# Layer 0's FFN: three pairs by token halves and eight by seven products, with six products ahead of the second projection and zeros between the convolution's additions

## The chip, the core and the metric

The kernel runs on one core of one Trainium2 chip. The core has five engines with a queue of instructions each: TensorE (PE, matmuls; its weight loads are shown as PEld), VectorE (DVE), ScalarE (ACT), GpSimd (POOL) and SyncE (SP, which here only issues DMAs). The metric is the device time in microseconds (us), the median of several runs. Lower is better.

## The reference

A two-layer decoder trunk on 512 tokens of width 1024, all in float32. Layer 0 is a causal convolution module and a SwiGLU FFN; layer 1 is sliding-window attention and the same kind of FFN. What matters here is layer 0:

```python
def swiglu_ffn(x, w_up, w_down):
    gate, up = jnp.split(x @ w_up, 2, axis=-1)
    return (jax.nn.silu(gate) * up) @ w_down

def conformer_conv(x, w_pw1, b_pw1, w_dw, b_dw, ln_g, ln_b, w_pw2, b_pw2):
    a = jax.nn.glu(x @ w_pw1 + b_pw1, axis=-1)
    y = lax.conv_general_dilated(
        a, w_dw[:, None, :].astype(a.dtype), window_strides=(1,),
        padding=((CONV_WIDTH - 1, 0),),
        dimension_numbers=('NWC', 'WIO', 'NWC'),
        feature_group_count=D_MODEL) + b_dw
    y = jax.nn.silu(layernorm(y, ln_g, ln_b))
    return y @ w_pw2 + b_pw2

h = x
h = h + conformer_conv(rmsnorm(h, norm_mix[0]), ...)
h = h + swiglu_ffn(rmsnorm(h, norm_ffn[0]), ffn_w_up[0], ffn_w_down[0])
...
```

The convolution is 31 taps wide. `w_up` is 1024 x 5632 and `w_down` 2816 x 1024, so the FFN's hidden width is 2816: 22 tiles of 128, which the kernel takes as 11 pairs.

## The kernel before, in words

**Layout.** Channels lie on the partitions, tokens along the free axis. `h` is eight tiles of 128 x 512. The tokens are also worked on as two halves of 256 (`HALF`).

**Weights.** All weights come as chunks of 128 x 1024 (512 KB) in one order, `PLAN`, made by `chunk_plan` (L92). SP loads a chunk into one of six `raw` buffers (`load`, L257), up to nine ahead. `split_weights` (L293) then splits it, three ahead, into a rounded part `whi` (ACT, L294) and the rest `wlo` (DVE, L297), with four buffers each, and a matmul of such operands is three (`mm3`, L376): whi by x's high part, whi by x's low part, wlo by x's high part, on L380 to L382. Chunks up to pair 0 of part 0 (`NATIVE`) aren't split (L378). `advance` (L299) does all of this and runs once for each chunk used; `get` (L362) calls it, and also `pace` (L337), which counts gets and brings background jobs as far as their points say. A point (get, step) means: so many steps by that get.

**Two ways through the FFN's up projection.** Before the change pairs 0 to 3 go *by token halves* (`HALVES0[0]`): `ffn_part` runs once for the first 256 tokens (part 0; three matmuls of 256 columns per step) and once for the second (part 1, `twin`; `mm2`, L407: one matmul of 512 columns, high and low parts side by side, and one of 256). Each part runs four up chunks per pair and, after all its pairs, two down chunks per pair. Pairs 4 to 10 go *by seven products* (Strassen-Winograd over two halves of the input channels and two halves of the tokens; `SEVEN`, L57): seven chunks per pair for all 512 tokens, each a `product` (L801) of 24 matmuls of 256 columns. Their weight blocks A11 to A22 are in memory; the sums S1 to S4 are made in DRAM by `prepare` (L277), a fraction `share[0]` of a sum per chunk: SP copies a block (`copy_sums`, L269; the first nine pairs' in bulk while the convolution runs), and POOL's DMA queue adds a second block onto it (L289). The token sums T1 to T4 are made by `Rows0.sums` (L1284). `SevenPair.take` (L818) evacuates each product into a tile `c`, and `gates` (L844) finishes the pair: DVE L849 and L852, silu on ACT L850, multiplication on POOL L853.

**Order of layer 0.** The convolution of the first token half; pw2 for it; part 0 (ups, then downs); three products A12 ahead of their pairs (`FIRST`: they need only the first half's tokens), kept in a `quad`; pw2 for the second half; part 1; the other products of pairs 4 to 10; all 14 of their down chunks; then the shared K/V projection.

**The second half's convolution** (`Half`, L976) runs in the background of pw2 and part 0. Taps are shared: DVE accumulates 14 to 16 of each channel tile's 31 (L1009); for the others ACT multiplies (L1001) and POOL adds (L1002). After the last tap POOL joins the two (L1013), ACT squares (L1038), PE sums over the channels (`sums`, L1058), `scales_a` turns the sums (PE L1067, then small DVE operations), `scales_b` makes the scales (POOL L1080, ACT L1085), `spread` broadcasts them (PE L1089), and `rows` makes the eight tiles z (DVE L1101 and L1102, ACT L1103, split L544 and L545), which the second pw2 reads. Each of these is a step of the job at L1243; 39 steps of taps are left when it starts, so the squares are step 40, the sums 44, the scales 45 and 46, the spread with the first row 49, the last row 56. The order on each engine is fixed when the kernel is built; `issue_after` keeps an instruction from being placed ahead of another.

Outputs of part 0's downs are added into `h` by L621 and L622, of part 1's by L604 to L607 (L606 on POOL), of the seven-product pairs' by L1356. An up pair of part 0 is evacuated by L659, L661, L662 and `split` (L544, L545).

Of the kernel before, what the change touches and what calls it, by code (L numbers as in the profile page):

```python
# [34 lines left out]
HALVES0 = ((0, 4), (4, 11))  # L35
FIRST = (4, 5, 6)
# [38 lines left out]
def part2_products():  # L75

    steps, held = [], []
    for pair in range(*HALVES0[1]):
# [13 lines left out]
def chunk_plan():  # L92
# [19 lines left out]
    plan.extend(("up0", *step) for step in part2_products())  # L112
    downs(*HALVES0[1])
# [96 lines left out]
def hybrid_trunk(ctx: ExitStack, tc: tile.TileContext, xT, W, prm_in, wdw_in, sinks, relb, onehot, fin, lead, out):  # L210
# [53 lines left out]

    def pool_op(op):
        pooled[0] = op.ins
        return op
# [107 lines left out]

    def mm3(out, w, x, start, stop, **kw):  # L376
# [4 lines left out]
        nc.tensor.matmul(out, w[0], x[1], start=False, stop=False, **kw)  # L381
        nc.tensor.matmul(out, w[1], x[0], start=False, stop=stop, **kw)  # L382
# [202 lines left out]
    def ffn_part(layer, part, xg, tok, rms, on_h=None, twin=False, plain=None):  # L585
# [3 lines left out]
        for g in range(2):  # L589
            if twin:  # L590
# [210 lines left out]
    def product(key, block, r, opens, closes=True):  # L801
# [131 lines left out]

    with tc.tile_pool(name="conv", bufs=2) as cv:
# [41 lines left out]
        class Half:  # L976
# [7 lines left out]
            def taps(self, ct, c):  # L984
# [9 lines left out]
                for i in range(nd):  # L994
                    while pi * nd < n_pool * (i + 1):
# [4 lines left out]
                        else:  # L1000
                            on_act = nc.scalar.mul(pr, a[:, j:j + W2], tap(j))  # L1001
                            on_pool = pool_op(nc.gpsimd.tensor_add(pr, acc, pr))  # L1002
# [105 lines left out]
            def background(self):  # L1108
# [24 lines left out]
                self.spread()  # L1133
# [109 lines left out]
        job(second, (base, 0), (base + 8, 19), (base + 13, 22), (base + 26, 40), (base + 30, 45), (base + 34, 50), (base + 35, h1.n_steps - early - 3))  # L1243
# [28 lines left out]
    class Rows0:  # L1272
# [11 lines left out]
        def sums(self):  # L1284
# [6 lines left out]
            for n, (name, t, f, a, b) in enumerate((  # L1291
# [12 lines left out]
                both = z0.tile([P, 2, 4, 256], F32R, tag="z0", name=uid("rows"), bufs=5)  # L1304
# [5 lines left out]
    z0 = part2.enter_context(tc.tile_pool(name="part2", bufs=5))  # L1310
    plain1 = z0.tile([P, KT, W2], F32, tag="z0", name=uid("plain1"), bufs=5)
# [7 lines left out]
    flush()  # L1319
# [3 lines left out]
    share[0] = 1 / 4  # L1323
    lo0, hi0 = HALVES0[1]
    hid0, open_pairs = [], {}
    left = [n for n, _ in part2_products()]
    for pair, a in part2_products():
        if pair not in open_pairs:
            c = z0.tile([P, 2, 2, 2, 256], F32, tag="z0", name=uid("up"), bufs=5)
            open_pairs[pair] = SevenPair("up0", pair, rows0, c, first.get(pair))  # L1330
        open_pairs[pair].take(a)
        left.remove(pair)
        if pair in left:
            continue
        c = open_pairs[pair].gates()
        if 2 * (pair - lo0) == len(hid0):
            if pair == hi0 - 1:
                q = quad()
                two = q[:, 0:2], q[:, 2:4]
            else:  # L1340
                two = quad(), quad()
            hid0 += [[d[:, k, :] for d in two] for k in range(two[0].shape[1])]
        for m in range(2):
            split([d.rearrange("p (s q) -> p s q", s=2) for d in hid0[2 * (pair - lo0) + m]], c[:, m, :, 0, :])
    part2.close()

    attn = ExitStack()
    at = attn.enter_context(tc.tile_pool(name="attn", bufs=2))
    job(chain(*(read_bias(*b) for b in ((0, 0), (0, 1), (1, 0)))), (seen[0], 0), (seen[0] + 10, 7))
    share[0] = 0.6  # L1350
    if True:
# [346 lines left out]
```

## Time and profile before

| | |
|---|---|
| median of 3 runs | 1043.42 us (1043.19 to 1044.5) |
| profiled execution | 1043.27 us, its span 1041.5 us |
| mean granted TensorE clock | 0.997 |
| busy share of the span: PE, PEld, DVE, ACT, POOL | 99%, 90%, 75%, 59%, 45% |
| DMA | 248.33 MB, mean 238 GB/s |

The profile is of one execution. A group's row gives line, engine, operation, names and shapes, the count, busy us and the mean ns of one, then the engine's idle time before these instructions and what ended it. The chain of waits is followed back from the last instruction; in order of time it shows when each piece starts and how long it holds the chain. The sums by stage give each engine's busy time in a stretch. Layer 0's stages by the trace: first pw2 from about 129 us, part 0 from 158, the three early products from 235, the second pw2 from 244, part 1 from 267, the seven products from 339, their downs from 474 to 550.

### The profile page before, as it was taken

What the parts mean: (1) busy time and instruction counts of PE and PEld (TensorE: products, weight loads), DVE (VectorE), ACT (ScalarE), POOL (GpSimd) and SP (SyncE); (2) the same over time, 40 slices, a digit from 0 to 9 for tenths busy, and PEclk for the clock granted to TensorE, in tenths of its full rate; (3) what the DMA queues carried; (4) which work ended last, traced back from release to release, by engine and by line L of the source; (5) the groups of instructions that cost most, each with busy time, mean ns of one, the idle gap of its engine ahead of it and who ended that gap; (6) DMA issues with size and microseconds to landing.
All of it is one profiled execution on the core that took longest, in us unless ns stands there. A gap on an engine that the chain in (4) does not pass through costs nothing.

```text
span 1041.5 us, 17709 instructions
## 1 busy us (share of the span) xinstructions
PE 1031.5 (99%) x6580; PEld 932.6 (90%) x6580; DVE 776.5 (75%) x1202; ACT 613.0 (59%) x1062; POOL 473.2 (45%) x569
## 2 busy tenths in 40 slices
PE   9999999999999999999999999999999999999996
PEld 8888889999988999998888877788989999898995
DVE  3999989978789777673536566678686877868777
ACT  3887798847776556552333565466655556554654
POOL 3999999930535233221214255405442334434134
PEclk9999999999999999999999999999999999999998
DMA  9999747999999988999969766955879988877742
GB/s 356 340 315 207 205 126 204 272 256 275 249 239 262 304 220 284 256 301 244 286 209 254 210 183 183 228 154 152 252 230 312 287 264 264 245 233 222 224 150 81
DMA packets 67282, 248.33 MB, mean 238 GB/s; under 512 B 7579, under 2 KB 13884, under 8 KB 66364
## 3 DMA queue, kind: packets, MB, share of 16 engines
q1 hardware_dynamic: 54236, 200.75, 55.9%
q0 software_dynamic: 12672, 46.14, 24.8%
q8 instruction: 51, 0.84, 0.3%
q10 hardware_dynamic: 288, 0.31, 0.1%
q14 instruction: 35, 0.29, 0.1%
HBM read 241.93 MB, written 97.52 MB: 326 GB/s over the span
## 4 chain that ended last, share of the span: by engine, by line
PE 98%; DMA 0%; DVE 0%; issue 0%; POOLq 0%; SPq 0%; POOL 0%; ACT 0%
PE bank L380 20%; PE bank L382 20%; PE bank L381 20%; PE bank L960 10%; PE bank L902 9%; PE bank L412 4%; PE bank L378 4%; PE bank L413 2%; PE bank L1441 1%; PE bank L1483 1%; PE bank L1470 1%; PE bank L1058 1%; PE bank L1607 1%; PE bank L948 1%; DMA both<-in_lead_dram 0%; PE bank L1562 0%
## 5 line engine op out<-in xcount | busy, mean ns | idle before, releaser
L297 DVE TENSOR_TENSOR wlo<-raw,whi 128x1024 fp32r<-128x1024 f32 x246 | 329.7, 1348 | 136.8 <-ACT whi L294 136.5
L294 ACT CAST whi<-raw 128x1024 fp32r<-128x1024 f32 x246 | 257.1, 1049 | 276.6 <-PE bank L381 194.1
L380 PE MATMUL bank<-quad,whi 128*128 128x256 f32 (+1 forms) x976 | 307.4, 317 | 0.0
L381 PE MATMUL bank<-quad,whi 128*128 128x256 f32 (+1 forms) x976 | 306.6, 315 | 0.0
L382 PE MATMUL bank<-quad,wlo 128*128 128x256 f32 (+1 forms) x976 | 305.7, 315 | 0.0
L380 PEld LDWEIGHTS bank<-quad,whi 128*128 128x128 f32 x976 | 185.5, 191 | 12.8 <-issue 1.6
L381 PEld LDWEIGHTS bank<-quad,whi 128*128 128x128 f32 x976 | 186.0, 191 | 11.9 <-issue 0.5
L382 PEld LDWEIGHTS bank<-quad,wlo 128*128 128x128 f32 x976 | 185.6, 191 | 11.8 <-issue 0.4
L853 POOL TENSOR_TENSOR up<-up 128x512 f32<-128x512 f32 x34 | 62.9, 1851 | 283.6 <-ACT up L850 283.6
L1002 POOL TENSOR_TENSOR pr<-pr,pr 128x256 f32<-128x256 f32 x208 | 155.4, 788 | 2.6 <-ACT pr L1001 2.5
L380 PE MATMUL bank<-rows,whi 128*128 128x256 f32 x488 | 138.0, 283 | 0.0
L381 PE MATMUL bank<-rows,whi 128*128 128x256 f32 x488 | 137.8, 282 | 0.0
L382 PE MATMUL bank<-rows,wlo 128*128 128x256 f32 x488 | 137.8, 282 | 0.0
L1009 DVE SCALAR_TENSOR_TENSOR bank<-apad,wdw,bank 128x256 f32<-128x256 f32 x248 | 112.4, 485 | 3.4
L1001 ACT ACTIVATE pr<-apad,wdw 128x256 f32<-128x256 f32 x208 | 98.3, 502 | 14.9 <-POOL pr L1002 13.1
L960 PE MATMUL bank<-quad,w 128*128 128x256 f32 x448 | 98.7, 380 | 0.0
L960 PEld LDWEIGHTS bank<-quad,w 128*128 128x128 f32 x448 | 84.9, 190 | 11.8 <-DVE bank L1009 0.2
L380 PEld LDWEIGHTS bank<-rows,whi 128*128 128x128 f32 x488 | 93.1, 191 | 0.3
L381 PEld LDWEIGHTS bank<-rows,whi 128*128 128x128 f32 x488 | 93.1, 191 | 0.3
L382 PEld LDWEIGHTS bank<-rows,wlo 128*128 128x128 f32 x488 | 93.0, 191 | 0.0
L491 POOL TENSOR_TENSOR tmp<-tmp,tmp 128x256 f32<-128x256 f32 (+1 forms) x28 | 26.8, 957 | 101.4 <-ACT tmp L487 96.2
L412 PE MATMUL bank<-quad,whi 128*128 128x512 f32 x168 | 59.7, 398 | 0.0
(230 smaller groups left out, 1635.9 us busy)
## 6 DMA issues: line engine op xcount, KB each, us to landing
raw<-in_W_dram SPq DMA_DIRECT2D x170, 512.0 KB, 5.7
raw<-sum SPq DMA_DIRECT2D x88, 512.0 KB, 5.4
sum<-in_W_dram SPq DMA_DIRECT2D x52, 512.0 KB, 6.2
sum<-in_W_dram POOLq DMA_DIRECT2D x44, 512.0 KB, 9.6
sum<-sum POOLq DMA_DIRECT2D x44, 512.0 KB, 8.5
sum<-in_W_dram SPq DMA_DIRECT2D x4, 3584.0 KB, 30.4
w<-in_W_dram SPq DMA_DIRECT2D x14, 512.0 KB, 8.6
sum<-in_W_dram SPq DMA_DIRECT2D x4, 1024.0 KB, 30.3
```

The lines of the kernel that those rows point to most:

```text
L294: on_act = nc.scalar.copy(hi, src).ins
L297: latest[:] = [on_act, lo_engine[0].tensor_sub(lo, src, f32(hi)).ins]
L380: nc.tensor.matmul(out, w[0], x[0], start=start, stop=False, **kw)
L381: nc.tensor.matmul(out, w[0], x[1], start=False, stop=False, **kw)
L382: nc.tensor.matmul(out, w[1], x[0], start=False, stop=stop, **kw)
L412: nc.tensor.matmul(first[2], first[0], first[1], start=start, stop=False)
L853: pool_op(nc.gpsimd.tensor_mul(gate, gate, c[:, m, :, 1, :]))
L902: nc.tensor.matmul(out, x, w[:, ws], start=first and e == 0 and i == 0, stop=e == 1 and i == 2, skip_group_check=True)
L960: mm = nc.tensor.matmul(self.pb[:, w * W2:(w + 1) * W2], w1_of(ct, w, k), x[k] if x else xg[k][:, tok], start=k == 0, stop=k == KT - 1)
L1001: on_act = nc.scalar.mul(pr, a[:, j:j + W2], tap(j))
L1002: on_pool = pool_op(nc.gpsimd.tensor_add(pr, acc, pr))
L1009: on_dve = nc.vector.scalar_tensor_tensor(yt if i == nd - 1 else c, src, tap(i), c if i else self.shift, op0=ALU.mult, op1=ALU.add)
```

## The change

Pair 3 goes by seven products, so that three pairs go by halves and eight by products. The products run in two groups of four pairs (`GROUPS0`), each followed by its own down chunks, with the outputs added into `h` after each. The products A12 of six pairs (3 to 8) instead of three run ahead of the second pw2, with two gets counted by `pace` in each; two of their results lie in a new pool `keep`. `part2`'s pool has four buffers instead of five, and the tile `c` of odd pairs is a `quad`. From the second half's job on, each POOL addition of the convolution, and L606, is followed by a memset of 128 x 64 zeros into a tile that nobody reads. The job's points are new, and its sums, scales and spread are not placed ahead of the last matmul of `mm3` (`stamp`). The shares of sums per chunk become 0.5 (was 0.45) ahead of the products and 0.45 (was 0.25) among them. `EARLY` follows from `PLAN`: eight units in the first bulk copy instead of seven, one in the second instead of two.

```diff
-HALVES0 = ((0, 4), (4, 11))
-FIRST = (4, 5, 6)
+HALVES0 = ((0, 3), (3, 11))
+GROUPS0 = ((3, 7), (7, 11))
+FIRST = tuple(range(3, 9))
...
-    plan.extend(("up0", *step) for step in part2_products())
-    downs(*HALVES0[1])
+    for group in GROUPS0:
+        plan.extend(("up0", *step) for step in part2_products(group))
+        downs(*group)
...
+    letting = []
+
     def pool_op(op):
         pooled[0] = op.ins
+        return op
+
+    def let_go(op):
+        if letting:
+            with tc.issue_after(op.ins):
+                pool_op(nc.gpsimd.memset(letting[0], 0.0))
         return op
...
-            nc.tensor.matmul(out, w[0], x, start=start, stop=stop)
+            stamp[0] = nc.tensor.matmul(out, w[0], x, start=start, stop=stop).ins
...
-        nc.tensor.matmul(out, w[1], x[0], start=False, stop=stop, **kw)
+        stamp[0] = nc.tensor.matmul(out, w[1], x[0], start=False, stop=stop, **kw).ins
...
-                    pool_op(nc.gpsimd.tensor_mul(t, t, rs_bc))
+                    let_go(pool_op(nc.gpsimd.tensor_mul(t, t, rs_bc)))
...
         for which in range(2):
+            if which and between is not None:
+                between()
...
-                            on_pool = pool_op(nc.gpsimd.tensor_add(pr, acc, pr))
+                            on_pool = let_go(pool_op(nc.gpsimd.tensor_add(pr, acc, pr)))
...
                 for n, (_, f) in enumerate(due):
-                    f()
+                    with tc.issue_after(stamp[0]):
+                        f()
...
-                self.scales_a()
+                with tc.issue_after(stamp[0]):
+                    self.scales_a()
...
-                self.spread()
+                with tc.issue_after(stamp[0]):
+                    self.spread()
...
-        job(second, (base, 0), (base + 8, 19), (base + 13, 22), (base + 26, 40), (base + 30, 45), (base + 34, 50), (base + 35, h1.n_steps - early - 3))
+        letting.append(cpool.tile([P, 64], F32, tag="letting", name="letting"))
+        job(second, (base, 0), (base + 8, 19), (base + 13, 22), (base + 24, 39), (base + 28, 43), (base + 29, 44), (base + 30, 44),
+            (base + 31, 46), (base + 33, 48), (base + 34, 49), (base + 37, h1.n_steps - early))
...
-        preparing[0], share[0] = prepare(), 0.45
+        preparing[0], share[0] = prepare(), 0.5
...
-        first = quad(F32)
-        first = {pair: first[:, n, :].rearrange("p (a s) -> p a s", a=2) for n, pair in enumerate(FIRST)}
+        first = [quad(F32)] + [keep.tile([P, 512], F32, tag="c11", name=uid("c11")) for _ in FIRST[4:]]
...
-            product(("up0", pair, "A12"), [[x0["ffn0"][4 + k][e][:, HALF[0]] for k in range(4)] for e in range(2)], r, True)
+            product(("up0", pair, "A12"), [[x0["ffn0"][4 + k][e][:, HALF[0]] for k in range(4)] for e in range(2)], r, True, pace)
...
-    job(rows0.sums(), (base + 11, 0), (base + 19, 8), (base + 26, 14), (base + 32, 17))
+    job(rows0.sums(), (base + 10, 0), (base + 16, 8), (base + 22, 12), (base + 27, 14), (base + 31, 17))
...
-    share[0] = 1 / 4
-    lo0, hi0 = HALVES0[1]
-    hid0, open_pairs = [], {}
-    left = [n for n, _ in part2_products()]
-    for pair, a in part2_products():
+    share[0] = 0.45
+    for group in GROUPS0:
+        lo0, hi0 = group
+        last = hi0 == HALVES0[1][1]
+        hid0, open_pairs = [], {}
+        left = [n for n, _ in part2_products(group)]
+        for pair, a in part2_products(group):
+            if pair not in open_pairs:
+                if pair % 2:
+                    c = quads.tile([P, 2, 2, 2, 256], F32, tag="quad", name=uid("up"))
...
+            pace()
+            open_pairs[pair].take(a)
...
         for g in range(2):
             banks = accs(512)
             down_group([(("down", 0, kp, g), 2 * (kp - lo0)) for kp in range(lo0, hi0)], lambda kt: hid0[kt], banks)
             for m in range(4):
                 nc.vector.tensor_add(h[g * 4 + m], banks[m], h[g * 4 + m])
-                nxt.on_h(g * 4 + m)
+                if last:
+                    nxt.on_h(g * 4 + m)
```

More of the change, by code (lines that the diff above doesn't have):

```diff
@@ L72, in blocks_of, with part2_products @@
     return [(kind, pair, n.split()[0]) for n in SEVEN]
-def part2_products():
+def part2_products(group):
     steps, held = [], []
-    for pair in range(*HALVES0[1]):
+    for pair in range(*group):
         names = [n.split()[0] for n in SEVEN]
@@ L799, in hybrid_trunk, with product @@
     PARTNER = dict(n.split() for n in SEVEN)
-    def product(key, block, r, opens, closes=True):
+    def product(key, block, r, opens, between=None):
         w = [x.rearrange("p (a k c) -> p a k c", a=2, k=4) for x in get_seven(*key)]
         for which in range(2):
+            if which and between is not None:
+                between()
             for k in range(4):
@@ L932, in norm_x @@
         return pb
+    kept = ExitStack()
+    keep = kept.enter_context(tc.tile_pool(name="keep", bufs=max(1, len(FIRST) - 4)))
     with tc.tile_pool(name="conv", bufs=2) as cv:
@@ L1248, in hybrid_trunk @@
         pw2(h0.z, n0)
-        preparing[0], share[0] = prepare(), 0.45
+        preparing[0], share[0] = prepare(), 0.5
         ffn_part(0, 0, x0["ffn0"], HALF[0], n0.rms, plain=plain)
-        first = quad(F32)
-        first = {pair: first[:, n, :].rearrange("p (a s) -> p a s", a=2) for n, pair in enumerate(FIRST)}
+        first = [quad(F32)] + [keep.tile([P, 512], F32, tag="c11", name=uid("c11")) for _ in FIRST[4:]]
+        first = {pair: t.rearrange("p (a s) -> p a s", a=2)
+                 for pair, t in zip(FIRST, [first[0][:, n, :] for n in range(4)] + first[1:])}
         for pair in FIRST:
@@ L1345, in hybrid_trunk @@
[L1345 to L1351, printed above, removed]
+    share[0] = 0.45
[8 more added lines that the diff above has]
+                    c = quads.tile([P, 2, 2, 2, 256], F32, tag="quad", name=uid("up"))
+                else:
+                    c = z0.tile([P, 2, 2, 2, 256], F32, tag="z0", name=uid("up"), bufs=4)
+                open_pairs[pair] = SevenPair("up0", pair, rows0, c, first.get(pair))
+            pace()
+            open_pairs[pair].take(a)
+            left.remove(pair)
+            if pair in left:
+                continue
+            c = open_pairs[pair].gates()
+            if 2 * (pair - lo0) == len(hid0):
+                if pair == hi0 - 1:
+                    q = quad()
+                    two = q[:, 0:2], q[:, 2:4]
+                else:
+                    two = quad(), quad()
+                hid0 += [[d[:, k, :] for d in two] for k in range(two[0].shape[1])]
+            for m in range(2):
+                split([d.rearrange("p (s q) -> p s q", s=2) for d in hid0[2 * (pair - lo0) + m]], c[:, m, :, 0, :])
+        flush()
+        if last:
+            part2.close()
+            kept.close()
+            attn = ExitStack()
+            at = attn.enter_context(tc.tile_pool(name="attn", bufs=2))
+            job(chain(*(read_bias(*b) for b in ((0, 0), (0, 1), (1, 0)))), (seen[0], 0), (seen[0] + 7, 7))
+            share[0] = 0.6
@@ L1356, in hybrid_trunk @@
                 nc.vector.tensor_add(h[g * 4 + m], banks[m], h[g * 4 + m])
-                nxt.on_h(g * 4 + m)
+                if last:
+                    nxt.on_h(g * 4 + m)
+    if True:
         x, rms = nxt.x, nxt.rms
```

25 lines of the change are left out of this document (4 added, 21 removed).

## The prediction

> **What bounds the kernel now.** I read the page first, then the chain of waits, then sums by stage.
>
> ```profile
> span 1041.5 us, 17709 instructions
> ...
> PE 1031.5 (99%) x6580; PEld 932.6 (90%) x6580; DVE 776.5 (75%) x1202; ACT 613.0 (59%) x1062; POOL 473.2 (45%) x569
> ...
> PE 98%; DMA 0%; DVE 0%; issue 0%; POOLq 0%; SPq 0%; POOL 0%; ACT 0%
> ```
>
> PE alone carries the chain. The profiled execution took 1043.27 us, 1.77 outside its span; the median of the runs is 1043.42, so the sum below is made against 1043.27. A busy PE row doesn't show how long one matmul holds the chain; the chain in order of time does (start, length):
>
> ```profile
> 396.29 0.12 PE bank L381
> 396.41 0.12 PE bank L382
> ...
> 399.17 0.12 PE bank L381
> ```
> ```profile
> 287.85 0.23 PE bank L412
> 288.08 0.12 PE bank L413
> 288.20 0.23 PE bank L412
> ```
> ```profile
> 479.20 0.23 PE bank L382
> ...
> 479.88 0.23 PE bank L382
> ```
>
> A 256-column matmul costs 0.12 us: a product (24 of them; the first and last row are 24 apart) 2.88. The token-half step of part 1 (512 and 256 columns, L412 and L413) costs 0.35, its chunk of eight 2.80. A 512-column matmul costs 0.68 / 3 = 0.227, a chunk of 24 of them 5.44. Nobody else bounds a stage, but two come near (columns: stretch, its length, then busy us of PE, PEld, DVE, ACT, POOL, then clock, DMA share, GB/s):
>
> ```profile
> 172.00:208.50 36.50, 36.50 (x300) 36.29 (x299) 34.23 (x47) 28.17 (x52) 34.66 (x39) 1.00 0.99 271
> 208.50:234.50 26.00, 26.00 (x212) 25.76 (x211) 19.33 (x30) 11.93 (x18) 8.29 (x10) 1.00 0.92 255
> 243.70:339.00 95.30, 95.30 (x616) 86.50 (x616) 82.59 (x106) 64.87 (x109) 36.66 (x37) 1.00 0.92 255
> 339.00:474.00 135.00, 135.00 (x1105) 133.76 (x1104) 96.51 (x109) 74.51 (x98) 35.66 (x26) 1.00 0.91 274
> 474.00:550.50 76.50, 76.50 (x339) 63.32 (x339) 33.63 (x34) 28.83 (x40) 18.40 (x20) 1.00 0.80 236
> ```
>
> From 172 to 208.5, where the second half's convolution runs under part 0 of the FFN, DVE is busy 94%, POOL 95%, and DMA is full. The granted clock is 1.00 throughout, so no clock term.
>
> **The PE sum.** Pair 3 leaves the halves. Part 0 loses four up and two down chunks, 6 x 2.88 = 17.28 (24 matmuls of 256 columns each, the product's price); part 1 loses 6 x 2.80 = 16.80. Added are seven products, 7 x 2.88 = 20.16, and two down chunks, 2 x 5.44 = 10.88. Sum: 31.04 - 34.08 = **-3.04 us**. The products A12 of pairs 7 and 8 only move forward; the cut into two groups adds no matmul. PE shows no idle to win back, so -3.04 is about the floor, and the question is what stalls come.
>
> **The tight place: the second half's LayerNorm.** Before the second pw2, part 0 gets 6 x 2.88 shorter and 3 x 2.88 longer: 8.64 us less cover for a chain that runs convolution, column sums, spread, z. Today's chain (four views; rows in time):
>
> ```profile
> 206.84 1.86 POOL L1002 TENSOR_TENSOR pr<-pr,pr 128x256 f32<-128x256 f32 x2
> 216.54 2.42 POOL L1013 TENSOR_TENSOR y<-y,pr 128x256 f32<-128x256 f32 x2 [7.84 <-DVE y L1009]
> ```
> ```profile
> 215.92 0.87 DVE L1009 SCALAR_TENSOR_TENSOR y<-apad,wdw,bank 128x256 f32<-128x256 f32 x2
> 251.83 0.75 DVE L545 TENSOR_TENSOR quad<-tmp,quad 128x256 fp32r<-128x256 f32 x2
> ```
> ```profile
> 219.00 0.42 ACT L1038 ACTIVATE sq<-y 128x256 f32<-128x256 f32 x1 [1.26 <-POOL y L1013]
> ```
> ```profile
> 220.31 1.73 PE bank L1058 x8
> 225.15 0.79 PE bank L1067 x8
> 234.44 0.86 PE bank L1089 x2
> ```
>
> POOL's additions end at 208.70 and then wait 7.84 for DVE, whose taps end at 216.79; 2.6 us on, at 219.42, the sums can start, and PE takes them at 220.31. The spread ends at 235.3, three products follow, and pw2 starts at about 243.9; its last z lands at 252.58, when the fourth pw2 chunk (243.9 + 8.64 = 252.5) begins. There is no room to spare today.
>
> After: pw2 starts at 243.9 - 8.64 = 235.3. Going back over five products (14.40), spread, scales and sums (0.86 + 0.79 + 1.73), the sums stand at 217.5, ahead of the second product. So the taps must be done by 217.5 - 2.6 = 214.9, 1.9 sooner than today. With the added gets (two per product) the steps run 1.55 per get instead of 1.38, and the taps end at get 24, one earlier. DVE's order up to there loses one weight split and pair 3's evacuation (L659, L662, L545) and takes in the first half of the down evacuation (L621 and L622, twice each), all like this row (columns here and next: count, busy, mean ns):
>
> ```profile
> L662 DVE TENSOR_TENSOR bank<-bank,tmp 128x512 f32<-128x512 f32 x4 | 2.7, 687 | 0.0
> L297 DVE TENSOR_TENSOR wlo<-raw,whi 128x1024 fp32r<-128x1024 f32 x18 | 28.1, 1572 | 2.1 <-ACT whi L294 2.1
> ```
> ```profile
> L297 DVE TENSOR_TENSOR wlo<-raw,whi 128x1024 fp32r<-128x1024 f32 x11 | 13.5, 1223 | 4.3 <-ACT whi L294 4.2
> ```
> ```profile
> L1002 POOL TENSOR_TENSOR pr<-pr,pr 128x256 f32<-128x256 f32 x40 | 38.1, 1010 | 1.8 <-ACT pr L1001 1.8
> ```
> ```profile
> L1002 POOL TENSOR_TENSOR pr<-pr,pr 128x256 f32<-128x256 f32 x34 | 23.5, 730 | 0.0
> ```
>
> That is -1.57 - 3 x 0.69 + 4 x 0.69 = -0.9: taps at 215.9, 1.0 too late if nothing else changes. The rows show what may change: a split takes 1.572 from 160 to 217, where POOL adds, but 1.223 from 240 to 270, where it doesn't; an addition takes 1.010 beside the splits and 0.730 from 100 to 125 without them. The two engines block each other; the splits alone lose 18 x 0.35 = 6.3 us. Zeros between the additions could let DVE in. The relief isn't measured: between 0 and 6.3; I take a third, 2.1, because a split that meets a running addition must still wait for it, and only double waits vanish. Then the taps end at 213.8 and the sums wait for nothing.
>
> By the Trainium skill (SBUF — State Buffer, § Who interferes with whom) a DVE instruction with two SBUF inputs contends with a GpSimd instruction that reads SBUF, not with one that only writes. The trace agrees as far as the split's two durations go, and by that rule alone the relief is whole: taps at 209.6, the total still the PE sum, 1040.2. The same page (§ SBUF: two separate sides) lets whichever starts first keep the pair for its whole instruction, which speaks against the change, since the zeros shorten no addition under way: relief near 0, which gives the third case below.
>
> POOL pays for the zeros. Of the 116 additions of this half, 54 are emitted early, so 62 get one (and eight in L606, off this chain). Of 64 columns there is no row; nearest are these (the second: seven of 30 columns, so (0.47 - 0.12) / 6 = 0.058 each):
>
> ```profile
> 1.08 0.20 POOL L469 MEMSET mean_m<- 128x128 f32 x1
> ...
> 1.81 0.47 POOL L937 MEMSET apad<- 128x30 f32 x7
> ```
>
> So 3.6 to 12.4 us; between the two by width, 0.107, makes 6.6: additions end at 215.3, and with two y additions of 0.73 and the square the sums are ready at 217.2 against 217.5. The 7.84 us of POOL idle are eaten almost whole. I allow **0.2 us** of PE waiting, here or at the z. The z: DVE needs about 8 us for eight rows (three steps of 0.33) with splits taking 1.22 of every 2.88, some 14 us from the spread's end (217.5 + 1.73 + 2.88 + 0.79 + 2.88 + 1.44 + 0.86 = 228.1), so 242.1, against 243.9 needed. Behind a late sum or spread, everything on PE queues, since its order is fixed.
>
> **The rest, hidden.** Eight more evacuations between the groups (0.69 each) lie under down chunks, where DVE is busy 33.63 of 76.5; uncovered, the next product would wait for a bank, at most four of them, 2.7 us. Three more PSUM copies on ACT replace others in part 2. T1 to T4 come at gets 17 to 29 instead of 20 to 32; the first product that needs one of them is get 28, and T4's own is get 33. Part 1 keeps DVE's 87%: six splits and a pair go with the time. The POOL multiplication that closes each group's last pair has three down chunks, 16 us, ahead of its use.
>
> DMA is where the change asks for more: sums at 0.45 per chunk in part 2 instead of 0.25 (SP's queue carries the loads and the copies, POOL's the accumulations). Between 120 and 560:
>
> ```profile
> q1 hardware_dynamic: 21839, 83.46, 53.1%
> q0 software_dynamic: 6912, 25.17, 32.3%
> ...
> raw<-in_W_dram SPq DMA_DIRECT2D x105, 512.0 KB, 5.9
> ```
> ```profile
> ACT whi L294 <- DMA raw<-in_W_dram: 4.4, 1, 4.4
> ```
>
> 512 KB cost 0.531 x 440 / 159 = 1.47 us of all DMA engines on q1, 0.323 x 440 / 48 = 2.96 on q0. Part 2 now needs 1.47 + 0.25 x 4.43 = 2.58 per 2.88, or 0.90, and the row says 0.91. After: 1.47 + 0.45 x 4.43 = 3.46, that is 1.20, in the second group's 26 products: 15 us behind at their end. Loads start it with six raw buffers full and four chunks split, over 20 us ahead, and the down chunks give it back; ACT waited only once for a load, though DMA stood at 0.99. I count nothing.
>
> **Forecast and rivals.** 1043.27 - 3.04 + 0.2 = **1040.4**. About 0.2%, 2.1 us, can be told from no change.
> 1. All but a little of the PE sum arrives: 1039.6 to 1041.3. Chance 0.56.
> 2. POOL becomes the last ahead of the sums: at 0.20 per zero the additions end at 221.1, the sums are ready at 223.0, PE waits 5.5: 1045.7, more if the zeros also slow the additions. Slower than before from a wait of 3.04, or about 0.16 per zero. For it speaks POOL's 95%, against it the short row of 30 columns. 0.15.
> 3. The zeros do not do what they are for: DVE stays blocked, the sums are 1.0 late, and the last z, which today lands as it is used, as much again: 1042.2. DVE's 94% speaks for it. 0.19.
> 4. DMA holds the loads in the second group: if the six raw buffers alone cover, six products (17.3) less a landing (5.9) and the two halves of a split (2.3) make 9, and 15 less 9 is 6: 1046.2. The full share speaks for it, the single wait against. 0.10.
>
> So faster 0.56, same 0.19, slower 0.25. The range is 1039.4 to 1046.5, which takes in most of the second and fourth; the first alone is 1039.6 to 1041.3.
>
> **What would show it.** The products at 2.88 and 50 of them in part 2; L1002's mean down from 1.010 or L297's from 1.572 under the convolution; zeros near 0.1 us; no PE gap ahead of L1058, L1067, L1089 and the second pw2; DMA share about 1 in the second group without ACT waiting for raw. A gap of over 1 us at one of these places, or at the weights in the second group, makes it wrong.

## The result, and the profile after

The changed kernel takes 1051.31 us (median of 6 runs, 1050.92 to 1052.44), the kernel before 1043.61 beside it: a ratio of 1.0076, with a 95% interval of 1.0063 to 1.0089. It is slower, by 7.7 us; 1040.4 was forecast. The profiled execution took 1051.06, 7.79 above that of before. Line numbers have moved: a weight split on DVE is now L307 (was L297), an addition of the convolution on POOL L1018 (L1002), an accumulation's issue L299 (L289), and the zeros are L276. The page of the changed kernel, its span, engines and chain:

```profile
span 1049.0 us, 17719 instructions
...
PE 1033.1 (98%) x6556; PEld 933.1 (89%) x6556; DVE 780.6 (74%) x1208; ACT 611.3 (58%) x1059; POOL 488.0 (47%) x643
...
PE 86%; DVE 5%; issue 3%; POOL 2%; ACT 2%; DMA 0%; POOLq 0%; ACTq 0%; DVEq 0%
```

PE has 24 matmuls fewer and is no longer alone on the chain of waits: DVE, POOL and ACT are on it for 9% of the span. The view of waits for PE, 120 to 560 us (us in total, times, longest), has no row in the kernel before and three after:

```profile
PE bank L541 <- ACT tmp L527: 2.9, 1, 2.9
PE bank L393 <- DVE quad L557: 2.7, 3, 2.2
PE bank L392 <- DVE up L844: 0.9, 1, 0.9
```

The first is under part 0, and so is the second but for 0.2 us in the second pw2; the third is at the start of part 2. The chain of waits ahead of the first (start, length):

```profile
178.69 0.70 POOL sq L1060
179.39 0.10 POOL letting L276
179.54 0.16 POOL letting L276
179.75 0.16 POOL letting L276
...
180.65 1.88 POOL sum L299 x2
182.52 0.16 POOL letting L276
182.68 0.69 POOL rs L519
...
183.70 0.39 ACT tmp L527
```

Part 0's RMS scale goes through four engines: DVE makes the mean square `ms` (L517), POOL a power of it, `rs` (L519), ACT a diagonal (L527), and PE spreads that (L541). POOL's rs stands in POOL's queue behind a group of six zeros and two accumulations (L299). DVE's ms was ready long before (first row); in the kernel before, rs (there L507, second row) ran 4 us earlier:

```profile
175.91 0.15 DVE L517 TENSOR_SCALAR ms<-bank 128x2 f32<-128x2 f32 x1
```
```profile
178.61 0.71 POOL L507 TENSOR_TENSOR rs<-ms,mhalf 128x2 f32<-128x2 f32 x1
```

So the first wait comes from POOL's queue: ms ended at 176.06, and rs held the chain from 182.68. DVE's timeline shows the second wait:

```profile
191.85 5.83 DVE L307 TENSOR_TENSOR wlo<-raw,whi 128x1024 fp32r<-128x1024 f32 x1
...
202.25 1.28 DVE L557 TENSOR_TENSOR quad<-bank,quad 128x512 fp32r<-128x512 f32 x2
```

One weight split took 5.83 us, and the low half of the last pair's gated rows (L557), behind it in DVE's queue, came 2.2 us late for its down chunk. What POOL did in those 5.83 us:

```profile
191.89 1.00 POOL L1018 TENSOR_TENSOR pr<-pr,pr 128x256 f32<-128x256 f32 x1
192.56 0.41 POOL L276 MEMSET letting<- 128x64 f32 x1
192.67 1.69 POOL L1018 TENSOR_TENSOR pr<-pr,pr 128x256 f32<-128x256 f32 x2
194.04 0.41 POOL L276 MEMSET letting<- 128x64 f32 x1
194.14 1.67 POOL L1018 TENSOR_TENSOR pr<-pr,pr 128x256 f32<-128x256 f32 x2
195.52 0.39 POOL L276 MEMSET letting<- 128x64 f32 x1
195.62 0.96 POOL L1018 TENSOR_TENSOR pr<-pr,pr 128x256 f32<-128x256 f32 x1
196.30 0.79 POOL L276 MEMSET letting<- 128x64 f32 x3
```

POOL had six additions ready and ran them one after the other, with a single zero at three of the five places between them. The split ended at 197.68; if it runs in one piece, its own 1.22 us (what a split takes undisturbed) began at about 196.5, when the last of the six ended. Waits were not all. Four windows of 3.413 us (length, busy us of PE, PEld, DVE, ACT, POOL, then clock):

```profile
180.23:183.64 3.41, 1.03 (x9) 0.83 (x7) 0.00 (x0) 0.25 (x1) 3.23 (x9) 1.00 0.84 198
183.64:187.05 3.41, 2.91 (x11) 2.73 (x12) 2.00 (x2) 3.41 (x7) 3.41 (x7) 0.50 1.03 187
200.71:204.12 3.41, 1.19 (x10) 1.14 (x10) 3.41 (x6) 3.41 (x8) 3.01 (x7) 1.00 0.96 247
204.12:207.53 3.41, 3.41 (x18) 3.41 (x17) 3.41 (x5) 1.90 (x4) 3.41 (x4) 0.50 0.68 223
```

After each long wait the granted clock fell to half for one window. PE's timeline shows it in the starts of the matmuls, 0.12 apart and then 0.21:

```profile
203.80 0.28 PE L393 MATMUL bank<-quad,whi 128*128 128x256 f32 x1
203.92 0.28 PE L394 MATMUL bank<-quad,wlo 128*128 128x256 f32 x1
...
204.60 0.42 PE L392 MATMUL bank<-quad,whi 128*128 128x256 f32 x1
204.81 0.41 PE L393 MATMUL bank<-quad,whi 128*128 128x256 f32 x1
```

The account of the profiled executions: -3.04 forecast for PE's work, +6.5 of waits, +3.16 at half clock (half of PE's 2.91 and 3.41) make +6.6 of the 7.79; the rest is in smaller pieces. From 160 to 217 us, by form (count, busy, mean ns, idle before):

```profile
L1018 POOL TENSOR_TENSOR pr<-pr,pr 128x256 f32<-128x256 f32 x40 | 40.3, 1209 | 0.4 <-ACT pr L1017 0.4
...
L307 DVE TENSOR_TENSOR wlo<-raw,whi 128x1024 fp32r<-128x1024 f32 x14 | 27.8, 1997 | 5.7 <-ACT whi L304 5.7
...
L276 POOL MEMSET letting<- 128x64 f32 x50 | 13.9, 278 | 1.0
```

Both means went up, from 1.572 and 1.010 us, where they were to come down.

### The profile page after: what moved, and what is told of

Same layout as the page of the kernel before. It is cut to its first block, busy times and chain, and to the rows that moved or that the text cites. A ratio compares the mean times of both kernels' runs of the same rounds, so it can differ in the third digit from the quotient of the medians.

```text
span 1049.0 us, 17719 instructions
## 1 busy us (share of the span) xinstructions
PE 1033.1 (98%) x6556; PEld 933.1 (89%) x6556; DVE 780.6 (74%) x1208; ACT 611.3 (58%) x1059; POOL 488.0 (47%) x643
## 4 chain that ended last, share of the span: by engine, by line
PE 86%; DVE 5%; issue 3%; POOL 2%; ACT 2%; DMA 0%; POOLq 0%; ACTq 0%; DVEq 0%
PE bank L393 19%; PE bank L392 19%; PE bank L394 19%; PE bank L916 9%; PE bank L976 7%; PE bank L424 3%; PE bank L425 2%; DVE wlo L307 2%; DVE bank L1025 2%; POOL pr L1018 1%; PE bank L1471 1%; PE bank L1513 1%; PE bank L1500 1%; ACT pr L1017 1%; PE bank L1637 1%
## 5 line engine op out<-in xcount | busy, mean ns | idle before, releaser
L307 DVE TENSOR_TENSOR wlo<-raw,whi 128x1024 fp32r<-128x1024 f32 x243 | 322.6, 1335 | 132.9 <-ACT whi L304 132.5
L304 ACT CAST whi<-raw 128x1024 fp32r<-128x1024 f32 x243 | 253.9, 1048 | 279.2 <-PE bank L393 196.7
L867 POOL TENSOR_TENSOR up<-up 128x512 f32<-128x512 f32 x36 | 67.3, 1870 | 325.1 <-ACT up L864 315.9
L1018 POOL TENSOR_TENSOR pr<-pr,pr 128x256 f32<-128x256 f32 x208 | 157.5, 821 | 1.1 <-ACT pr L1017 1.1
L392 PE MATMUL bank<-rows,whi 128*128 128x256 f32 x512 | 144.8, 283 | 0.9 <-DVE up L844 0.9
L394 PE MATMUL bank<-rows,wlo 128*128 128x256 f32 x512 | 144.6, 282 | 0.0
L393 PE MATMUL bank<-rows,whi 128*128 128x256 f32 x512 | 144.6, 282 | 0.0
L392 PEld LDWEIGHTS bank<-rows,whi 128*128 128x128 f32 x512 | 97.6, 191 | 1.4 <-issue 1.1
L393 PEld LDWEIGHTS bank<-rows,whi 128*128 128x128 f32 x512 | 97.6, 191 | 0.3
L394 PEld LDWEIGHTS bank<-rows,wlo 128*128 128x128 f32 x512 | 97.6, 191 | 0.0
L916 PE MATMUL bank<-wlo,fhi 128*128 128x512 f32 x140 | 55.2, 394 | 0.0
```

Source lines behind the costliest of these rows:

```text
L304: on_act = nc.scalar.copy(hi, src).ins
L307: latest[:] = [on_act, lo_engine[0].tensor_sub(lo, src, f32(hi)).ins]
L394: stamp[0] = nc.tensor.matmul(out, w[1], x[0], start=False, stop=stop, **kw).ins
L867: pool_op(nc.gpsimd.tensor_mul(gate, gate, c[:, m, :, 1, :]))
L916: nc.tensor.matmul(out, x, w[:, ws], start=first and e == 0 and i == 0, stop=e == 1 and i == 2, skip_group_check=True)
L1018: on_pool = let_go(pool_op(nc.gpsimd.tensor_add(pr, acc, pr)))
```

## The experiments

Every kernel was timed beside the kernel before on the same chip, which took 1044.6 to 1044.9 in these runs; differences between kernels are read from the ratios. "Split" is the mean and the longest weight split from 160 to 217 us; "waits" is PE's waiting from 120 us to the end of the second pw2; "half" counts windows of 3.413 us at half clock there. The last three are of the profiled execution. a_noadds and b_noadds leave work out, so their results are not the reference's; all others compute everything.

| kernel | median us | ratio to before (95% interval) | split, us | waits | half |
|---|---|---|---|---|---|
| before | 1043.61 | | 1.57, 3.45 | 0 | 0 |
| changed | 1051.31 | 1.0076 (1.0063 to 1.0089) | 2.00, 5.83 | 5.6 | 2 |
| a_nozeros | 1051.51 | 1.0067 (1.0055 to 1.0080) | 2.30, 5.48 | 6.2 | 1 |
| b_zeros | 1052.15 | 1.0075 (1.0061 to 1.0089) | 2.35, 5.62 | 6.2 | 2 |
| a_share45 | 1045.83 | 1.0011 (1.0002 to 1.0020) | 1.75, 3.98 | 2.0 | 1 |
| a_nozeros45 | 1045.76 | 1.0013 (1.0004 to 1.0022) | 1.79, 4.73 | 1.9 | 1 |
| a_pinned | 1045.83 | 1.0013 (1.0002 to 1.0023) | 1.58, 3.35 | 2.8 | 0 |
| a_late | 1047.45 | 1.0024 (1.0015 to 1.0033) | 1.89, 5.21 | 3.6 | 1 |
| a_noadds | 1041.94 | 0.9974 (0.9963 to 0.9984) | 1.22, 1.23 | 0.2 | 0 |
| b_noadds | 1043.43 | 0.9985 (0.9975 to 0.9995) | 1.22, 1.23 | 0 | 0 |
| c13 | 1053.84 | 1.0082 (1.0068 to 1.0096) | 1.51, 4.35 | 7.9 | 5 |
| c14 | 1053.68 | 1.0087 (1.0073 to 1.0101) | 1.53, 3.77 | 5.7 | 1 |
| c13r | 1052.04 | 1.0072 (1.0059 to 1.0086) | 1.52, 4.35 | 8.0 | 2 |
| b13 | 1047.84 | 1.0025 (1.0017 to 1.0034) | 1.36, 1.78 | 2.4 | 0 |
| y_nozeros | 1046.42 | 1.0018 (1.0009 to 1.0027) | 1.61, 3.12 | 4.0 | 0 |
| y_nozeros45 | 1045.87 | 1.0008 (0.9999 to 1.0017) | 1.83, 3.44 | 2.1 | 1 |
| y_nozeros40 | 1046.40 | 1.0015 (1.0007 to 1.0024) | 1.88, 4.04 | 2.8 | 1 |
| y_before | 1043.31 | 0.9989 (0.9980 to 0.9998) | 1.74, 3.43 | 0 | 0 |
| b_share5 | 1048.25 | 1.0031 (1.0019 to 1.0043) | 1.98, 5.72 | 3.6 | 1 |

**Zeros or accumulations.** a_nozeros leaves the zeros out (the first diff below); b_zeros is the kernel before with the zeros alone; a_share45 has one number undone (the second diff); a_nozeros45 has both.

```diff
-        letting.append(cpool.tile([P, 64], F32, tag="letting", name="letting"))
```
```diff
-        preparing[0], share[0] = prepare(), 0.5
+        preparing[0], share[0] = prepare(), 0.45
```

> The changed kernel without POOL's zeros, all else kept. The changed kernel lost about 8.9 us ahead of the second half's pw2: two PE waits under part 0 (3.03 at the spread of part 0's RMS, 2.38 at the first down chunk), some 0.8 of small ones, and two stretches of 3.413 us at half the clock behind the two long waits, 1.7 us each. Theory Z (the zeros are the cause: in POOL's queue ahead of the RMS scale, and in slowing the additions): both waits and both half-clock stretches go, and the PE sum stands: 1040.3 to 1042. Theory A (the accumulations at 0.5 per chunk in POOL's queue are the cause, zeros a small part): the two accumulations are still ahead of the RMS scale, the first wait stays at 1.5 to 2.5, 1046 to 1050. Theory D (more convolution steps per get keep DVE and POOL blocking each other): the first wait goes, the second (2.4, at the low half of the quad) stays with its half-clock stretch: 1044.5 to 1046.

> The kernel before with POOL's zeros behind its additions and nothing else of the change. Theory Z: the RMS scale of part 0 and the additions move later, a PE wait of over 1 us appears under part 0, with a half-clock stretch behind it: 1045.5 to 1050. Theories A and D: the zeros run in POOL's idle time, no PE wait over 0.5 us: 1043 to 1044.2. If the zeros do what they are for, the splits under the convolution come down from 1.572 us towards 1.223.

> The changed kernel with the accumulations of part 0 at 0.45 per chunk as before instead of 0.5 (about one fewer in twenty chunks), the zeros kept. Theory A: one accumulation instead of two stands ahead of the RMS scale, the first wait (3.03) falls to 0 to 1.5 and its half-clock stretch goes: 1045.5 to 1048. Theory Z and D: both waits stay: 1049.5 to 1052.

> The changed kernel without zeros and with the accumulations of part 0 at 0.45, as before. POOL's order ahead of the RMS scale is then close to that of before, with accumulations between the y additions. Theory L: what decides is where POOL's run of additions meets a split, which shifts with every small change; with accumulations spread as before the 5.48 us split at 171 us goes and the RMS wait with it: 1042 to 1046. If the zeros are what makes 0.45 good (1045.8 with them): 1049 or more.

No theory had all of this right: a_share45 came out in theory A's range and a_nozeros45 in theory L's, a_nozeros and b_zeros outside every range. In the changed kernel the zeros make no difference that can be told (ratio 1.0076 with, 1.0067 without; 1.0011 and 1.0013 at 0.45), but put into the kernel before they cost 0.75%, 7.8 us. The accumulations' rate costs 0.65% with and 0.54% without zeros, 6.8 and 5.6 us. So neither edit has a price of its own. What goes along with the time is the longest split and PE's waits. The timelines of a_nozeros, POOL's and DVE's, show how two accumulations do it without a zero:

```profile
170.22 1.88 POOL L299 DMA_DIRECT2D sum<-in_W_dram  x2
171.50 2.04 POOL L1029 TENSOR_TENSOR y<-y,pr 128x256 f32<-128x256 f32 x2
172.88 2.04 POOL L1018 TENSOR_TENSOR pr<-pr,pr 128x256 f32<-128x256 f32 x2
174.26 1.34 POOL L1059 TENSOR_TENSOR yy<-y 128x256 f32<-128x256 f32 x1
174.96 2.38 POOL L1060 TENSOR_TENSOR sq<-sq,sq 128x256 f32<-128x256 f32 x1
180.55 1.63 POOL L519 TENSOR_TENSOR rs<-ms,mhalf 128x2 f32<-128x2 f32 x1 [3.21 <-DVE ms L517]
```

```profile
169.61 8.82 DVE L307 TENSOR_TENSOR wlo<-raw,whi 128x1024 fp32r<-128x1024 f32 x3
178.35 2.05 DVE L1025 SCALAR_TENSOR_TENSOR bank<-apad,wdw,bank 128x256 f32<-128x256 f32 x4
180.32 0.15 DVE L517 TENSOR_SCALAR ms<-bank 128x2 f32<-128x2 f32 x1
```

The same three splits in the kernel before:

```profile
169.70 5.18 DVE L297 TENSOR_TENSOR wlo<-raw,whi 128x1024 fp32r<-128x1024 f32 x3
```

At 0.45 one accumulation stands ahead of the two y additions and one behind them; at 0.5 both stand ahead, and six additions follow without a break. Three splits then take 8.82 us instead of 5.18 before, ms and the RMS scale come late behind them, and PE waits. So this wait has another cause than the changed kernel's at the same place: here rs waits for DVE, there it stood in POOL's queue. Over the 13 traces that have all or most of these additions and no other break in them, I counted the places between two POOL operations on SBUF (the core's working memory) while a split waited: with nothing between, the split got in at 32 of 86; with one zero between, at 17 of 41; with an accumulation's issue between, at 12 of 13. Where such a place begins and ends is a matter of judgement (wider bounds give 41 of 98, 23 of 47 and 16 of 17). Either way a split gets in at fewer than half of the places with nothing between, and a single zero hardly helps.

**Zeros in their places.** a_pinned holds every addition behind the zeros of the one before, so that they alternate; a_late does so at 0.45, with zeros only from part 0 on.

```diff
-                            on_pool = let_go(pool_op(nc.gpsimd.tensor_add(pr, acc, pr)))
+                            with tc.issue_after(zeroed[0]) if zeroed else nullcontext():
+                                on_pool = let_go(pool_op(nc.gpsimd.tensor_add(pr, acc, pr)))
```

> The changed kernel with each addition of the convolution held behind the zeros of the one before it, so that the zeros alternate with the additions instead of collecting in groups of three to seven. If it is the groups that delay the RMS scale and that leave the additions back to back against DVE: the first wait falls below 1.5, the longest split falls from 5.83 us to under 3.5, and the time is 1041 to 1046. If zeros between additions give DVE nothing and only lengthen POOL's work: 1049 or more, with the splits' mean unchanged.

> The changed kernel with the accumulations of part 0 at 0.45, with zeros strictly alternating with the additions, and with no zeros before part 0 begins (ahead of the RMS scale three zeros stand among its last nine POOL operations). Theory L with the queue: the wait at the spread of the RMS (2.4 in the run with alternating zeros) falls below 1.2, the others stay under 0.5: 1042 to 1044. If the wait there comes from a blocked split ahead of the RMS's ms on DVE and not from POOL's queue: it stays at 1.5 or more, 1044.5 to 1047.

a_pinned came out in its good half (longest split 3.35), though its wait at the RMS stayed at 2.3. a_late lost that wait, as expected, but its time lies above both of its ranges: a split of 5.21 us, with a zero between any two of the additions that held it, made PE wait 2.9 at another chunk. So alternating zeros don't by themselves keep a split from waiting. Why a_pinned does 0.63% better than the changed kernel is not shown; its longest split got in at about 186.6, where POOL issued an accumulation, so luck with the places is my reading.

**The additions away.** Both kernels without the 62 additions:

```diff
-                            on_pool = let_go(pool_op(nc.gpsimd.tensor_add(pr, acc, pr)))
+                            on_pool = on_act if quiet else pool_op(nc.gpsimd.tensor_add(pr, acc, pr))
```

> The changed kernel without zeros and without the 62 POOL additions of the second half's convolution that are emitted from part 0 on (these products are left out of the sum). Theory L (a split on DVE waits until POOL's run of additions is broken, and that alone costs the time ahead of the second pw2): no split over 1.3 us and no PE wait from 175 to 245 us, so the PE sum arrives but for the wait of about 1 us at the start of part 2: 1040.0 to 1041.8. Rival Q (the accumulations in POOL's queue or DMA's full share delay the loads and the RMS scale): a PE wait of over 1 us stays under part 0, 1043 or more.

> The kernel before without the same 62 additions. The kernel before shows no PE wait under part 0, so it can gain nothing: 1042.5 to 1044.5 by every theory. Its difference from the changed kernel without the additions is the change without the struggle of POOL and DVE: theory L expects -3.0 + 1.0 = about -2, rival Q 0 or above.

The view by form of a_noadds, 160 to 217 us, and its waits of PE from 120 to 560:

```profile
L307 DVE TENSOR_TENSOR wlo<-raw,whi 128x1024 fp32r<-128x1024 f32 x17 | 20.8, 1221 | 3.6 <-ACT whi L304 3.5
```

```profile
PE bank L392 <- ACT whi L304: 1.1, 1, 1.1
PE bank L393 <- DVE quad L557: 0.2, 1, 0.2
```

This settles the first question: without POOL's additions every split takes 1.22, accumulations at 0.5 and DMA as full as before, and nothing waits under part 0. So neither the accumulations nor a full DMA makes PE wait by itself, and rival Q falls in that form. POOL's queue is not cleared by this run, which has no zeros and a nearly idle POOL (5.72 of 36 us busy from 172 to 208): in the changed kernel the first wait does come from that queue. The time of a_noadds is 0.14 us above theory L's range. The difference of the two is -1.5 us by the medians and about -1.1 by the ratios, each ratio being good to about 1 us; the change without the struggle should give -3.04, and +1.3 for the two waits above, together -1.7. b_noadds gains 0.15% on the kernel before, where nothing was to be gained; what that is stays open.

**Fewer additions, more taps.** If splits and additions exclude each other, four or eight additions fewer should make room. c13 and c14 move taps from ACT and POOL to DVE; c13r also has the T sums at the old pace; b13 is the kernel before with the same.

```diff
-N_POOL = ((13, 13, 12, 12), (17, 15, 15, 15))
+N_POOL = ((13, 13, 12, 12), (17, 15, 13, 13))
```

> The changed kernel without zeros, accumulations at 0.45, and in the second half's last two pairs of channel groups 13 taps each on ACT and POOL instead of 15 (eight additions fewer on POOL, 0.7 us each, eight taps more on DVE, 0.48 us each, no computation left out). Theory L as a budget: splits (1.22 us each when undisturbed) and POOL's additions (0.70 each back to back) exclude each other; in the kernel before 18 splits and some 45 additions make 22 + 31 = 53 of the 57 us from 160 to 217, so 8.64 us less cover cannot hold them. With 5.6 us less of additions the waits under part 0 go: 1041.5 to 1043. Rival: DVE, 94% busy, is the bound for itself, and 3.8 us more of taps make it late: sums late by 2 or more, 1045.5 or more.

> The same with 14 taps instead of 13 (four additions fewer, four taps more on DVE). Budget: half the relief, one wait of up to 1.5 us may be left: 1042 to 1045. Rival: 1045.5 or more.

> As the run with 13 taps, and the sums of rows T1 to T4 under part 1 at the pace of the kernel before, later by about one weight chunk. All runs with the change waited 1.07 to 1.28 us at the second product of part 2, behind DVE's evacuation of the first. If DVE's earlier T sums cause this, it falls below 0.5 and the time is 0.6 to 1.2 below that of the run with 13 taps; if it comes from the first product opening on six banks still being evacuated, nothing changes, or a later product waits for T4.

> The kernel before with 13 taps in those two pairs. It had no PE wait under part 0 in its profile, so 1042.5 to 1044.5: the relief is worth something only with the change. If it is as fast as the run with 13 taps of the changed kernel, the change brings nothing of its own.

My budget failed; c13, c14 and b13 are slower than its ranges. Under part 0 c13 has no wait left, but its column sums came 7.2 us late (in c14, with half the taps moved, 4.0); c13's wait of PE there, and the stretch ahead (PE, PEld, DVE, ACT, POOL, clock):

```profile
PE bank L1074 <- POOL y L1029: 7.2, 1, 7.2
```

```profile
206.00:227.00 21.00, 14.32 (x120) 14.12 (x118) 20.78 (x34) 7.25 (x8) 0.35 (x2) 0.90 0.83 222
```

DVE is busy 20.78 of 21.00 us there while POOL has nearly nothing to do: DVE's own work is the second limit. In c13 a split of 4.35 us just ahead has a part in it, but b13, whose longest split is 1.78, still loses 2.4 us at its spread. c13r shows that the wait at the start of part 2 (1.1 in all of these) is not due to the pace of the T sums; what makes it stays open.

**POOL's runs cut short.** The work is left as it is, and POOL waits for every split under part 0, so at most four additions stand between two splits.

```diff
             latest[:] = [on_act, lo_engine[0].tensor_sub(lo, src, f32(hi)).ins]
+        if yielding:
+            yielded[:] = [pool_op(nc.gpsimd.tensor_copy(yielding[0], f32(lo)[:, 0:1])).ins]
...
+                            with tc.issue_after(yielded[0]) if yielded else nullcontext():
+                                on_pool = pool_op(nc.gpsimd.tensor_add(pr, acc, pr))
```

> The changed kernel without zeros (1051.5) and, under part 0, a copy of one column on POOL behind every weight split that reads the split's result: the additions emitted behind a split wait until it is done, so at most four stand between two splits. Theory L (a split waits for the end of POOL's run of additions): no split over 3.5 us instead of 5.48, 4.54 and 5.35, no PE wait over 1 us under part 0, and 1042.5 to 1046. Rival W (DVE's own work is too much for the shorter time): the waits only move, to the weights or to the sums: 1048 or more.

> The same copies in the changed kernel without zeros and with the accumulations at 0.45 (1045.8, with a split of 4.73 us and a PE wait of 1.9 behind it). Theory L: that split goes below 3.5 and the wait and its half-clock stretch go: 1041.8 to 1043.5, ahead of the kernel before. Rival W: 1045 or more.

> The same copies in the kernel before, whose longest split there is 3.45 us and whose weights come 1.39 us ahead of their use at the tightest. Theory L: that margin grows by a us or more, and the time stays within 1.5 us of the kernel before (nothing waits there in its profile): 1043 to 1045. If POOL's waits make the additions and with them the sums late: 1046 or more.

On the worst kernel this takes off 0.49%, 5.1 us, though POOL has more to do; the longest split falls from 5.48 to 3.12 and no window is at half clock. Two waits of over 1 us are left, where none was expected:

```profile
PE bank L545 <- ACT tmp L531: 1.7, 1, 1.7
PE bank L396 <- ACT quad L560: 1.4, 1, 1.4
```

On the milder one nothing is gained: the longest split falls to 3.44, but PE waits 1.3 for the gated rows of the last pair and 0.8 more, with the half clock behind. y_before misses too: its tightest weight comes 0.38 us ahead of its use, not over 1.39, yet it is the fastest kernel of the study that leaves nothing out, 0.02 to 0.20% ahead of before, which is barely clear of the noise. Cutting the runs heals the long splits; it does not win back DVE's time.

**The rate alone, and less of it.** b_share5 is the kernel before at 0.5 per chunk; y_nozeros40 is y_nozeros45 at 0.4.

```diff
-        preparing[0], share[0] = prepare(), 0.45
+        preparing[0], share[0] = prepare(), 0.5
```

> The kernel before with the accumulations of part 0 at 0.5 per chunk instead of 0.45 and nothing else. On POOL two accumulations then stand together ahead of two y additions, as in the changed kernel without zeros, where a split waited 5.48 us behind the unbroken run that follows. If the rate alone does it: a split of over 4.5 us near 171 us, a PE wait at the RMS's spread, 1047 to 1051. If it needs the three pairs: 1043.5 to 1045.5.

> The changed kernel without zeros, with the copies that make POOL wait for each split, and accumulations at 0.4 per chunk in part 0. If the accumulations' place in POOL's queue still decides: the waits of 1.5, 0.6 and 0.4 us at the first down chunks and the half-clock stretch behind them shrink: 1042 to 1044. If those waits come from the shorter part itself (the last pair's gated rows are used two down chunks after their up chunk, not three): 1045 to 1047.

The rate alone costs the kernel before 3.3 us (1048.25 beside 1044.91), with the same three splits at 170 us (8.86), the RMS wait (1.4) and another split of 5.72 us. Fewer accumulations than 0.45 bring nothing: a split of 4.04 us holds PE for 2.3.

## Why the prediction was wrong

**The PE sum was right.** 50 products stand in part 2, 2.87 us apart; a_noadds beside b_noadds has the -3.04 but for two waits that the rows name, as far as the noise of about 1 us lets one see.

**The step that failed first was one left out.** "Sums at 0.45 per chunk in part 2 instead of 0.25" was costed; the same line of the diff in part 0, 0.45 to 0.5, was not. It is one accumulation more in twenty chunks, and the sum has no term for it. Its price is 5.6 to 6.8 us in the changed kernel, 3.3 in the kernel before, not by its own time but by where it leaves POOL without a break. It is not the whole error: at 0.45 the changed kernel is still 1.1 to 1.4 us slower than before, with and without zeros, where -2.8 was forecast.

**The term that was too small is the 0.2 us of PE waiting.** It measured 5.6 ahead of and in the second pw2, 0.9 at the start of part 2, and 3.16 at half clock. "No PE gap ahead" was asked at the wrong places: I followed the chain to its end (sums, spread, z) and counted 8.64 us less cover there. The stalls came on the way, at the RMS spread and at a down chunk. The kernel before shows how near it was; the timelines of DVE and of PE:

```profile
196.13 1.61 DVE L297 TENSOR_TENSOR wlo<-raw,whi 128x1024 fp32r<-128x1024 f32 x1
```

```profile
199.13 0.28 PE L380 MATMUL bank<-quad,whi 128*128 128x256 f32 x1
```

A split ends at 197.74, and its chunk begins at 199.13: 1.39 us to spare. A split that waits one addition more than usual is covered, one that waits five is not.

**Relief by zeros, "a third, 2.1".** It is 0 in the changed kernel, and negative in the kernel before. The zeros did not even stand between the additions: `issue_after` holds a zero behind its addition, but not the next addition behind the zero, so additions stayed side by side and zeros collected in groups. And the argument had a split wait for one running addition; it can wait for several ready ones in a row. The Trainium skill (SBUF — State Buffer, § SBUF: two separate sides) has the pair held "for the whole instruction"; here six additions, one after the other, held up a split whose row starts at 191.85, just ahead of the first of them. Its other rule (§ Who interferes with whom), by which an instruction that only writes doesn't contend, let me expect an opening at each zero; the runs show 17 of 41. The third rival (the zeros do not do what they are for, DVE stays blocked) had the blocking right, but not the place (PE never waited for the sums), and its price, 1.0 us late, was far too small. The zeros' own price was summed at 0.107 us. In the chain above a zero right behind an addition holds 0.10 us; in the group of six ahead of rs one takes 0.16, and the next starts 0.21 after it.

**"The granted clock is 1.00 throughout, so no clock term."** True of the kernel before, which never waits. A long wait brings a term of its own, 1.5 and 1.7 us here behind waits of 2.9 and 2.2.

**Pricing the rest.** Neither the fourth rival nor the second (POOL last ahead of the sums) came. For the fourth, the DMA sum asked for 1.20 in the second group; the share was 0.90 from 432.7 to 504 us, and no load was waited for. One wait of 0.9 to 1.1 us at the start of part 2 was not foreseen.

## What to carry to other kernels

Where DVE and POOL both work on SBUF, don't price POOL's work by its busy time: look for the longest run of POOL instructions that have their inputs ready, and compare it with the smallest time that a DVE result is ahead of its use. Look at what stands ahead of POOL's small results, too. When that margin is near one instruction, a small edit that moves POOL's order, even a DMA issue, can cost more than the work that the change saves, as it did here. And a wait of about 1.7 us or more on PE can carry a stretch at half clock behind it, which cost about 1.7 us more.

## What was not expected of the hardware

The half clock follows windows of 3.413 us that keep their phase through an execution: the two in the changed kernel begin at 183.64 and 204.12, six windows apart. In all the traces together there are 17 windows, between 150 and 400 us, with PE idle for 1.70 us or more, and after 16 of them the clock was at half (the other: 1.79, in b_zeros); after none with 1.55 or less did it fall from full to half. So it matters where a wait lies. In a_pinned PE waited 2.3 us and paid nothing more, because the wait was cut by the border of two windows (PE busy is the first number behind the length, the clock the 1.00):

```profile
178.87:182.28 3.41, 2.46 (x21) 2.26 (x19) 2.60 (x4) 2.28 (x5) 3.41 (x7) 1.00 1.00 298
182.28:185.70 3.42, 2.11 (x16) 2.06 (x17) 1.69 (x2) 2.86 (x6) 3.42 (x9) 1.00 1.05 243
```

In a_share45 a wait of 1.8 us inside one window cost 1.7 more. The Trainium skill (TensorE: Matmul & The Clock Gate, § Part 1: The HAM clock gate) gives a free-running window of 3413 ns, and the traces agree; it lets the clock fall after an idle window, and here half a window was enough.
